# A hybrid mixer on one core: the rest of the input projection placed between the steps of the recurrence, and two attention stages given their own banks

## The chip, the cores and the metric

The kernel runs on one core of a Trainium2 chip. The metric is the device time of one execution in microseconds (us). Engines are named as in the profile: PE is TensorE (matrix products; PEld its weight loads), DVE is VectorE, ACT ScalarE, POOL GpSimd, SP SyncE, which issues most DMAs. PEclk is the share of TensorE's full clock that was granted.

## The reference, cut to what matters

One layer: 1024 latent and 256 context tokens, width 1024. The normalised tokens go through one input projection, whose columns feed three mixers side by side: a bidirectional recurrence (4 heads), a neighbourhood attention (8 heads) and a gated short convolution. Their outputs are concatenated and projected; then an expert mixer of 16384 experts follows.

```python
pc = split_columns(hc @ w_in)          # 256 context tokens
pl = split_columns(hl @ w_in)          # 1024 latent tokens
y_rw_c, y_rw_l = rwkv_mixer(pc, pl, ...)
y_na_l = neighbourhood_attention(ql, kl, vl, kc, vc, na_rpb)
y_sc_l = gated_short_conv(*pl[9:12], sc_conv_w)
yl = jnp.concatenate([y_rw_l, y_na_l, y_sc_l], axis=-1) @ w_out
...
xl = xl + g1 * yl
hl2 = rmsnorm(xl, norm2_g[i]) * (1.0 + sc2) + sh2
xl = xl + g2 * peer_ffn(hl2, ...)      # query projection, top-16 of keys, gathered or dense experts
```

The recurrence reads only the first nine column blocks of the projection (128 columns each), the attention and the convolution the other eighteen.

## The kernel before, in words

**Order of the work.** The program is written through a layer that puts each engine's instructions in an order of its own: what is written earlier has precedence, and what is written later fills in where an engine would be free and its buffers are there. Each engine then runs its own queue strictly in that order. So the place at which a piece of work is written decides where it stands in the queues.

**Projection.** `proj(m, blk, evac)` makes column block m for a block of tokens (`TBLK`: 0 with 256 tokens, 256 and 768 with 512 each). It loads 512 KB of weights, casts them on ACT into a rounded part `wh` (L206), subtracts on POOL for the rest `wl` (L208), and runs 8 x 3 products on PE into a tile `pj` (L158 to L160). The result goes to DRAM. `load_h` brings a block's normalised tokens back and splits them the same way (`hbh` on ACT L188, `hbl` on POOL L189). The loads of weights, of tokens and of modulation rows (`awT`) share two buffers.

**Recurrence.** `batch(step, d)` handles 256 tokens in direction d: for two pairs of heads the decays (`th`, `de`, `di`, `pe`, `pi`), on POOL `bb` and `kb` (L533, L534), 64 x 64 products on PE (all on L460: `pk`, `pr`, `tr`, `lkv`), then a triangular inverse, which starts with 15 steps of small DVE instructions (`yb`, `Y`, L576 to L580) and ends in `XT`, and last the chain of states (`mc`, `M`, `yc`). Ten batches are written one after the other; the projections that the recurrence itself needs (`rwkv_inputs`) stand between the first of them. The last use of a token block also normalises and writes the output (`y`, `yd`, `yo`). `yc` and `yo` have the only bank of kind ch.

**The other projections.** `head_inputs` (12 projections of a latent block, 8 of the context) and `conv_inputs` (6) are written after the recurrence, for block 256 and then 0, and in the trace some of them already run in its gaps. Those of block 768 are written much later, after group 0.

**Attention.** `attend` goes through heads and query blocks of 128 tokens. An item is: scores `pw` and `pc` on PE, maximum on DVE (L778 to L781), two exponentials on ACT (L782, L783), transposes `pt` on PE (L792), copies `pT` on ACT, the products `po` (L798), and a scaling `yn` on DVE (L799). Query blocks 0 and 1 come first, with all PSUM tiles in the two banks of kind pj; then group 0 (output projection of the first 256 tokens, normalisation, query projection of the experts, sorting of the keys' scores on DVE, L922 to L926); then query blocks 2 to 5, with every second item followed by a projection of block 768, and beside them the first 30 gathered expert rows (`ru`, DVE L1118); then the convolution, group 1, and the expert products up to the end.

Of the kernel before, what the change touches and what calls it, by code (L numbers as in the profile page):

```python
# [25 lines left out]
TBLK = ((0, 256), (256, 512), (768, 512))  # L26
# [28 lines left out]
def hybrid_kernel(ctx: ExitStack, tc: tile.TileContext, A: dict, out: bass.AP, dbg=None):  # L55
# [7 lines left out]
    def pool(name, bufs=1, side="left"):  # L63
        return tc.tile_pool(name=name, bufs=bufs, side=side, reuse_waits="tile")
# [106 lines left out]
    def drain(gen):  # L171
        for _ in gen:
            pass
# [288 lines left out]
    def batch(step, d):  # L462
# [14 lines left out]
        for h in range(2):  # L477
# [86 lines left out]
            for u in range(4):  # L564
# [3 lines left out]
            S[h] = dict(E=EL[:, :, 0, :], bn=G[:, :, 0, :], bp=G[:, :, 1, :], bb=G[:, :, 0:2, :], kt=G[:, :, 2, :], gk=G[:, :, 3, :],  # L568
                        rx=rx, krd=krd, vS=vS, tot=tots, gt=gt)

        nc.vector.tensor_copy(Y, id16.unsqueeze(1).to_broadcast([P, 8, 16]))
# [12 lines left out]
        for u in range(8):  # L584
            heads2(ps[:, u * 64:u * 64 + 64], (XT[:, u, :], stk))
        nc.scalar.copy(X, v8(ps))

        for l in range(2):
            ps = bank(f"lp_{step}{d}{l}", "rb")
            for u in range(8):  # L590
                heads2(ps[:, u * 64:u * 64 + 64], (S[u // 4]["E"][:, u % 4, :], X[:, u, :]))
            pm = gp.tile([P, 8, 64], F32, tag="pm", name=f"pm_{step}{d}{l}", bufs=2)
            nc.vector.tensor_mul(pm, v8(ps), mask(C_L16 + l, 8))
            ps = bank(f"lt_{step}{d}{l}", "rb")
            for u in range(8):
                heads2(ps[:, u * 64:u * 64 + 64], (pm[:, u, :], XT[:, u, :]))
            if l == 0:
                ps2 = bank(f"lx_{step}{d}{l}", "rb")
                for u in range(8):
                    heads2(ps2[:, u * 64:u * 64 + 64], (XT[:, u, :], pm[:, u, :]))  # L600
                nc.vector.tensor_add(X, v8(ps2), X)
            nc.vector.tensor_add(XT, v8(ps), XT)
        for h in range(2):
            s, ci = S[h], 2 * d + h
            x12 = s["gt"]("x12", [P, 4, 2, 64], 4)
            ps = bank(f"x12_{step}{ci}", "rb")
            for u in range(4):
                heads2(ps[:, u * P:(u + 1) * P], (XT[:, 4 * h + u, :], s["rx"][:, u].rearrange("p a b -> p (a b)")))
            nc.scalar.copy(x12, ps.rearrange("p (c a b) -> p c a b", c=4, a=2))
            s["x12"] = x12  # L610
        for h in range(2):
            s, ci = S[h], 2 * d + h
            pr = s["gt"]("pr", [P, 4, 2, 64], 4)
            na_ = 2 if lat else 1
            ps = bank(f"pr_{step}{ci}", "rb")
            for u in range(4):
                heads2(ps[:, u * P:u * P + 64 * na_], (s["x12"][:, u, 0, :], s["bb"][:, u, :na_, :].rearrange("p a b -> p (a b)")))
            nc.vector.tensor_add(pr[:, :, :na_, :], ps.rearrange("p (c a b) -> p c a b", c=4, a=2)[:, :, :na_, :], s["krd"][:, :, 0:na_, :])
            s["pr"] = pr

        ych = bank(f"yc_{step}{d}", "ch") if lat else None
# [55 lines left out]
        nc.sync.dma_start(d_y[:, 0:2, tl:tl + 256], gs)  # L677

    batch(0, 0)
    batch(0, 1)  # L680
    rwkv_inputs(TBLK[1])
    batch(1, 0)
    load_h(*TBLK[2], 0)
    rwkv_inputs(TBLK[2])
    batch(1, 1)
    for step in range(2, 5):
# [3 lines left out]
    st_c.close()  # L690


    left = iter(range(16, 48))
    load_h(*TBLK[1], 1)
    drain(head_inputs(TBLK[1], 3))
    drain(conv_inputs(TBLK[1]))
    load_h(*TBLK[0], 1)
    drain(head_inputs(TBLK[0], 2))
    st_w.close()
# [111 lines left out]

    with pool("na", 2, "right") as na:
        drain(attend(na, range(0, 2), 0, 512, ("pj", "pj", "pj", "pj"), (2, 2, 1, 2, 1)))
    st_k = ExitStack()
    tk = st_k.enter_context(pool("tk", 1, "right"))

    st_i = ExitStack()
# [24 lines left out]
    def group(gi, tp_, eng):  # L842
# [23 lines left out]
        def to_rows(dst, t0, nt):  # L866
            for tt in range(nt):
                for q in range(2):
                    ps = bank(f"xt{gi}{tt}{q}", "ra")
                    for j in range(4):  # L870
# [4 lines left out]

        pq = bank(f"s2{gi}", "ra")[:, :n]
        for k in range(KD):
# [19 lines left out]
        for hp2 in range(16):  # L897
# [7 lines left out]
            nc.scalar.copy(qh, ps)  # L905
            ps = bank(f"sc{gi}{hp2}", "ra")
            for tt in range(nt):
# [257 lines left out]

    st_w = ExitStack()
    W[0] = st_w.enter_context(pool("wst2", 2, "right"))
    WT[:] = du, ("u", "uh", "ul"), 3
    with pool("tp") as tp_:
# [4 lines left out]
        drain(topk(0, 4, 4))  # L1174
    load_h(*TBLK[2], 2)

    def heads():
        hin = itertools.chain(head_inputs(TBLK[2]), conv_inputs(TBLK[2]))
        for i in range(4):
            yield next(hin)  # L1180
        with pool("nb1") as na:
            for i, ev in enumerate(attend(na, range(2, 6), 0, 1024, ("ra", "rb", "ch", "ra"), (3, 2, 1, 1, 1))):
                yield ev
                if i % 2:
                    next(hin, None)

    beside(heads(), 36, *PACE["b1"])
    st_w.close()
    conv(256, TL)
# [260 lines left out]
```

## Time and profile before

| | us |
|---|---|
| median of 3 runs (lowest to highest) | 3749.64 (3747.22 to 3761.19) |
| the profiled execution | 3754.22 |
| its span, from the first to the last instruction | 3752.5 |
| PE busy | 3329.1 (89%) |
| DVE busy | 2810.7 (75%) |
| ACT busy | 1529.2 (41%) |
| POOL busy | 1378.3 (37%) |

Busy time is a mean over stages with different limits, so the stages are read one by one: the busy time of each engine in a stretch, the groups of instructions in it by source line and tile (with count, busy us, mean ns of one, the idle time of the engine before them and what ended it), and a tile's own row, with the shortest, median and longest duration and the start of the first and last. In names, `out<-in` are the program's tiles. PE's matrix products overlap each other, so many of them take less time than their mean duration times their count.

### The profile page before, as it was taken

To read this page: it belongs to the slowest core of one execution; us is meant where nothing else is said; L and a number is where in the kernel's file an instruction comes from. 1 tells how busy PE (TensorE), PEld (TensorE's weight loads), DVE (VectorE), ACT (ScalarE), POOL (GpSimd) and SP (SyncE) were. 2 spreads that over 40 slices of the span, in tenths; PEclk is the share of its full clock that TensorE was granted. 3 is DMA by queue.
4 is the path that set the end of the run, shared out by engine and by line. 5 is a ranking of instruction groups with operands and counts; after the bars stand their busy time and mean duration, and the time that the engine had idled before them with its cause. 6 is when DMAs were issued, how large, how long until landed. Compare 5 with 4: busy or idle time off the path is not lost.

```text
span 3752.5 us, 63457 instructions
## 1 busy us (share of the span) xinstructions
PE 3329.1 (89%) x23959; PEld 2970.6 (79%) x23959; DVE 2810.7 (75%) x6095; ACT 1529.2 (41%) x2934; POOL 1378.3 (37%) x1060
## 2 busy tenths in 40 slices
PE   7787877857879887989989999999988999999997
PEld 6576776645768766888989999999987788888886
DVE  6553657433495656979879999999877788888888
ACT  3443222223434433336443676666632323323332
POOL 3333111220044223355442425565443344444444
PEclk9899988965789878989999999999999999999998
DMA  6435422252366644699977879999999999999997
GB/s 246 134 96 154 122 83 71 84 174 70 105 199 180 183 161 162 221 325 302 328 265 258 296 253 361 352 354 368 347 356 308 329 342 350 339 352 333 338 353 244
DMA packets 405811, 928.56 MB, mean 247 GB/s; under 512 B 45568, under 2 KB 182144, under 8 KB 399872
## 3 DMA queue, kind: packets, MB, share of 16 engines
q1 hardware_dynamic: 248064, 408.81, 33.8%
q0 software_dynamic: 111920, 407.95, 30.2%
q10 hardware_dynamic: 45520, 107.76, 7.5%
q8 instruction: 188, 3.08, 0.3%
q14 instruction: 119, 0.97, 0.1%
HBM read 802.74 MB, written 121.63 MB: 246 GB/s over the span
## 4 chain that ended last, share of the span: by engine, by line
PE 33%; DVE 14%; issue 6%; DMA 5%; ACT 2%; POOL 1%; SPq 0%; ACTq 0%; DVEq 0%; POOLq 0%
PE dp L158 5%; PE dp L160 5%; PE dp L159 5%; DVE ru L1118 4%; PE ds L160 3%; PE ds L158 3%; PE ds L159 3%; PE dq L158 2%; PE dq L159 2%; PE dq L160 2%; PE gm L1033 2%; DMA ru<-in_peer_u_dram,idx 1%; DVE acc L1129 1%; DVE ob L1025 1%; DVE oa L1020 1%
## 5 line engine op out<-in xcount | busy, mean ns | idle before, releaser
L1101 POOL DMA_INDIRECT ru<-in_peer_u_dram,idx x384 | 515.2, 1342 | 740.8 <-ACT dqs L1353 171.8
L1101 POOL DMA_INDIRECT rv<-in_peer_v_dram,idx x384 | 511.5, 1332 | 688.6 <-ACT dqs L1353 228.3
L1118 DVE CUSTOM_DVE_ANT_0 ru<-ru,h 128x1024 f32<-128x1024 f32 x384 | 478.6, 1259 | 83.0 <-DMA ru<-in_peer_u_dram,idx 81.0
L1129 DVE SCALAR_TENSOR_TENSOR acc<-rv,gw,acc 128x1024 f32<-128x1024 f32 x381 | 488.9, 1283 | 38.9 <-DMA rv<-in_peer_v_dram,idx 32.7
L159 PE MATMUL dp<-dvls,dwhs 128*128 128x512 f32 x896 | 348.5, 389 | 1.1 <-DVE dvls L1235 1.1
L160 PE MATMUL dp<-dvhs,dwls 128*128 128x512 f32 x896 | 345.8, 389 | 0.0
L158 PE MATMUL dp<-dvhs,dwhs 128*128 128x512 f32 x896 | 316.9, 392 | 0.0
L208 POOL TENSOR_TENSOR wl<-w,wh 128x1024 fp32r<-128x1024 f32 x68 | 165.9, 2442 | 284.5 <-ACT wh L206 273.9
L158 PE MATMUL pj<-hbh,wh 128*128 128x512 f32 (+1 forms) x544 | 225.7, 415 | 43.7 <-ACT wh L206 30.7
L160 PE MATMUL pj<-hbh,wl 128*128 128x512 f32 (+1 forms) x544 | 219.3, 403 | 7.7 <-POOL wl L208 7.6
L159 PE MATMUL pj<-hbl,wh 128*128 128x512 f32 (+1 forms) x544 | 220.0, 404 | 3.7 <-POOL hbl L189 3.7
L1268 ACT ACTIVATE ge<-ds 128x256 f32<-128x256 f32 (+1 forms) x256 | 110.8, 433 | 235.4 <-PE ds L160 190.7
L1238 ACT CAST dwhs<-dws 128x640 fp32r<-128x640 f32 x128 | 91.7, 730 | 260.4 <-DVE dws L1237 129.6
L158 PEld LDWEIGHTS dp<-dvhs,dwhs 128*128 128x128 f32 x896 | 169.7, 189 | 35.2
L159 PEld LDWEIGHTS dp<-dvls,dwhs 128*128 128x128 f32 x896 | 168.3, 188 | 36.6 <-DVE dvls L1235 1.5
L160 PEld LDWEIGHTS dp<-dvhs,dwls 128*128 128x128 f32 x896 | 168.3, 188 | 35.0
L158 PE MATMUL dq<-dvhs,dwhs 128*128 128x512 f32 x384 | 150.9, 393 | 19.3 <-ACT dvhs L1234 15.2
L158 PEld LDWEIGHTS pj<-hbh,wh 128*128 128x128 f32 x544 | 114.6, 211 | 66.6 <-ACT wh L206 31.6
L1235 DVE TENSOR_TENSOR dvls<-dvs,dvhs 128x1024 fp32r<-128x1024 f32 x128 | 155.7, 1221 | 10.7 <-ACT dvhs L1234 10.0
L1033 PE MATMUL gm<-oa,ob 128*128 128x128 f32 x1280 | 158.5, 277 | 5.7 <-DVE oa L1020 5.2
L1033 PEld LDWEIGHTS gm<-oa,ob 128*128 128x128 f32 x1280 | 154.0, 193 | 7.2 <-issue 7.0
L1353 ACT COPY dqs<-dq 128x512 f32<-128x512 f32 x90 | 52.8, 586 | 257.4 <-PE dq L160 257.4
(1984 smaller groups left out, 10156.9 us busy)
## 6 DMA issues: line engine op xcount, KB each, us to landing
du<-in_peer_ut_dram SPq DMA_DIRECT2D x128, 512.0 KB
dvs<-in_peer_v_dram SPq DMA_DIRECT2D x128, 512.0 KB
d_ge<-ge ACTq DMA_DIRECT2D x128, 320.0 KB
d_g<-gt ACTq DMA_DIRECT2D x40, 1024.0 KB
dgs<-d_g SPq DMA_DIRECT2D x32, 1280.0 KB
dws<-d_ge SPq DMA_DIRECT2D x128, 320.0 KB
w<-in_w_in_dram SPq DMA_DIRECT2D x68, 512.0 KB
wq<-in_q_w_dram SPq DMA_DIRECT2D x48, 512.0 KB
```

Of the source, the lines that this page charges most:

```text
L158: nc.tensor.matmul(ps, lh_, rh_, start=start, stop=False)
L159: nc.tensor.matmul(ps, lh_, rl_, start=False, stop=False)
L160: nc.tensor.matmul(ps, ll_, rh_, start=False, stop=stop)
L208: WE[0].tensor_tensor(wl, w, wh.bitcast(F32), op=OP.subtract)
L1033: nc.tensor.matmul(ps[:, t * P:(t + 1) * P], ob[:, q + t], oa[:, q + t], start=True, stop=True)
L1101: paced(nc.gpsimd.indirect_dma_start(out=r, out_offset=None, in_=A[tab], in_offset=bass.IndirectOffsetOnAxis(ap=idx[:, tt, s:s + 1], axis=0)))
L1118: yield from rows("peer_u", tt, lambda s, u: nc.vector.tensor_tensor_reduce(u, u, h2, 1.0, 0.0, OP.mult, OP.add, act[:, s:s + 1]))
L1129: nc.vector.scalar_tensor_tensor(acc, v, w[:, s:s + 1], acc, op0=OP.mult, op1=OP.add)
L1235: sv = nc.vector.tensor_tensor(vl, v, vh.bitcast(F32), op=OP.subtract)
L1238: nc.scalar.copy(wh, wt)
L1268: ev = nc.scalar.activation(ge[:, t0:t0 + n], ps, AF.Gelu_apprx_tanh)
L1353: pace[0] = nc.scalar.copy(dqs[:, r % 2], ps)
```

## The change

- `others()` makes one sequence of all remaining projections: block 768 first (its tokens are still in place, so one reload goes), then 256, then 0. `fill()` takes the next of them, and `batch` calls it six times: after each pair of heads, after `x0`, after each of the two steps that complete the inverse, and after `pr`. It works from batch (1, 1) on, seven batches, so 42 of the 44 projections are written inside the recurrence; what is left follows it. The modulation rows are spread anew over them (2, 1 and 2 a call instead of 3 and 2), 32 as before.
- The attention of query blocks 0 and 1 gets its own space (its pool is opened after the pool `tk` of the sorting instead of giving its space to it), three score buffers instead of two, and banks of three kinds: ra for scores, pj for transposes, ch for outputs.
- Group 0 uses the two banks of kind rb throughout, where it had three ra banks as well.
- The attention of query blocks 2 to 5 no longer alternates with projections, and has its transposes in pj instead of rb, in a pool on the other side of memory. It is paced as 32 pieces instead of 36.

```diff
             S[h] = dict(E=EL[:, :, 0, :], ...)
+            fill()
...
         nc.scalar.copy(X, v8(ps))
+        fill()
...
             nc.vector.tensor_add(XT, v8(ps), XT)
+            fill()
...
             s["pr"] = pr
+        fill()
...
+    left = iter(range(16, 48))
+    def others():
+        for blk, na, i in ((TBLK[2], 2, None), (TBLK[1], 1, 1), (TBLK[0], 2, 1)):
+            if i is not None:
+                load_h(*blk, i)
+            yield from head_inputs(blk, na)
+            if blk[0]:
+                yield from conv_inputs(blk)
+    rest, fill = others(), lambda: None
...
     rwkv_inputs(TBLK[2])
+    fill = lambda: next(rest, None)
     batch(1, 1)
...
-    left = iter(range(16, 48))
-    load_h(*TBLK[1], 1)
-    drain(head_inputs(TBLK[1], 3))
-    drain(conv_inputs(TBLK[1]))
-    load_h(*TBLK[0], 1)
-    drain(head_inputs(TBLK[0], 2))
+    drain(rest)
...
-    with pool("na", 2, "right") as na:
-        drain(attend(na, range(0, 2), 0, 512, ("pj", "pj", "pj", "pj"), (2, 2, 1, 2, 1)))
     st_k = ExitStack()
     tk = st_k.enter_context(pool("tk", 1, "right"))
+    with pool("na", 2, "right") as na:
+        drain(attend(na, range(0, 2), 0, 512, ("ra", "pj", "ch", "ra"), (3, 2, 1, 2, 1)))
...
-        pq = bank(f"s2{gi}", "ra")[:, :n]
+        pq = bank(f"s2{gi}", "ra" if gi else "rb")[:, :n]
...
-    load_h(*TBLK[2], 2)
     def heads():
-        hin = itertools.chain(head_inputs(TBLK[2]), conv_inputs(TBLK[2]))
-        for i in range(4):
-            yield next(hin)
-        with pool("nb1") as na:
-            for i, ev in enumerate(attend(na, range(2, 6), 0, 1024, ("ra", "rb", "ch", "ra"), (3, 2, 1, 1, 1))):
-                yield ev
-                if i % 2:
-                    next(hin, None)
-    beside(heads(), 36, *PACE["b1"])
+        with pool("nb1", 1, "right") as na:
+            yield from attend(na, range(2, 6), 0, 1024, ("ra", "pj", "ch", "ra"), (3, 2, 1, 1, 1))
+    beside(heads(), 32, *PACE["b1"])
```

What the change makes of the queues is seen at three places. The first is POOL in the recurrence, between the two pairs of heads of batch (2, 1); `bb_210` and `bb_211` belong to the first and the second pair, and a `wl` with the number of its column block to a projection. Before:

```order
L533 TENSOR_TENSOR bb_210_4170<-x2_210_4148,pi_210_4161 128x256
L534 TENSOR_TENSOR kb_210_4171<-x4_210_4149,pi_210_4161 128x256
L208 TENSOR_TENSOR wl10_7493<-w10_7489,wh10_7491 128x1024
L510 MEMSET de_301_4856 128x4
L510 MEMSET di_301_4857 128x4
L533 TENSOR_TENSOR bb_211_4288<-x2_211_4266,pi_211_4279 128x256
```

And now:

```order
L533 TENSOR_TENSOR bb_210_4654<-x2_210_4632,pi_210_4645 128x256
L534 TENSOR_TENSOR kb_210_4655<-x4_210_4633,pi_210_4645 128x256
L208 TENSOR_TENSOR wl20_4375<-w20_4371,wh20_4373 128x1024
L208 TENSOR_TENSOR wl12_4466<-w12_4462,wh12_4464 128x1024
L208 TENSOR_TENSOR wl23_4741<-w23_4737,wh23_4739 128x1024
L208 TENSOR_TENSOR wl25_4891<-w25_4887,wh25_4889 128x1024
L208 TENSOR_TENSOR wl21_4992<-w21_4988,wh21_4990 128x1024
L510 MEMSET de_301_5617 128x4
L510 MEMSET di_301_5618 128x4
L533 TENSOR_TENSOR bb_211_4805<-x2_211_4783,pi_211_4796 128x256
```

Five projections' subtractions stand ahead of the second pair's `bb`, where one stood.

The second place is PE at the start of the attention of query blocks 0 and 1; the first digit behind a name is the head, the second the query block. Before, the second item's scores stand behind the first one's products:

```order
L792 MATMUL pt014_8450<-cst2_95,s01_8425 128x128 x2
L798 MATMUL po01_8454<-vN00_8366,pT01_8443 128x64 x6
L772 MATMUL pw10_8481<-kh10_8463,qs10_8465 128x256
L773 MATMUL pw10_8481<-kl10_8473,qs10_8465 128x256
L776 MATMUL pc10_8484<-kh10_8463,qs10_8465 128x256
```

Now two items' scores stand together, between products of the recurrence's last batch (`yc`, `mc`):

```order
L460 MATMUL yc_41_8732<-x12_411_8660,G_411_8288 64x64 x2
L782 MATMUL pw00_9027<-kh00_9009,qs00_9011 128x256
L786 MATMUL pc00_9030<-kh00_9009,qs00_9011 128x256
L782 MATMUL pw01_9066<-kh00_9009,qs00_9011 128x256
L783 MATMUL pw00_9027<-kl00_9019,qs00_9011 128x256
L787 MATMUL pc00_9030<-kl00_9019,qs00_9011 128x256
L786 MATMUL pc00_9030<-kh00_9009,qs00_9011 128x256
L787 MATMUL pc00_9030<-kl00_9019,qs00_9011 128x256
L783 MATMUL pw01_9066<-kl00_9019,qs00_9011 128x256
L460 MATMUL yc_41_8732<-M_333_7093,pr_410_8671 64x64 x2
```

The third place is PE in group 0's query projection, at the end of `q00` and its scores `sc00`. Before, another query projection stands beside it:

```order
L159 MATMUL q00_9648<-hl0_9592,wq00h_9644 128x256
L160 MATMUL q00_9648<-hh0_9591,wq00l_9646 128x256
L159 MATMUL q01_9702<-hl0_9592,wq01h_9698 128x256
L160 MATMUL q01_9702<-hh0_9591,wq01l_9700 128x256
L908 MATMUL sc00_9677<-keys00_9673,qh00_9675 128x128 x2
L158 MATMUL q02_9752<-hh0_9591,wq02h_9748 128x256
```

Now items of the attention of query blocks 2 to 5 stand between the two:

```order
L159 MATMUL q00_10281<-hl0_10225,wq00h_10277 128x256
L160 MATMUL q00_10281<-hh0_10224,wq00l_10279 128x256
L808 MATMUL po12_11449<-vN0256_11217,pT12_11437 128x64 x4
L802 MATMUL pt130_11480<-cst2_95,s13_11461 128x128 x3
L808 MATMUL po12_11449<-vN0256_11217,pT12_11437 128x64 x3
L802 MATMUL pt130_11480<-cst2_95,s13_11461 128x128
L802 MATMUL pt134_11486<-cst2_95,s13_11461 128x128 x3
L782 MATMUL pw22_11617<-kh2256_11599,qs2256_11601 128x384
L918 MATMUL sc00_10310<-keys00_10306,qh00_10308 128x128 x2
L158 MATMUL q01_10335<-hh0_10224,wq01h_10331 128x256
```

On DVE, from the weights of group 1's fourth output block (`wo13l`) on, the rows are those of before with hardly a difference. Lines of the changed kernel are ten higher than those of before in the attention and group 0.

More of the change, by code (lines that the diff above doesn't have):

```diff
@@ L868, in to_rows @@
                 for q in range(2):
-                    ps = bank(f"xt{gi}{tt}{q}", "ra")
+                    ps = bank(f"xt{gi}{tt}{q}", "ra" if gi else "rb")
                     for j in range(4):
@@ L905, in group @@
             nc.scalar.copy(qh, ps)
-            ps = bank(f"sc{gi}{hp2}", "ra")
+            ps = bank(f"sc{gi}{hp2}", "ra" if gi else "rb")
             for tt in range(nt):
@@ L1164, in beside @@
         gbase[0] = g0 + ng
-    st_w = ExitStack()
-    W[0] = st_w.enter_context(pool("wst2", 2, "right"))
-    WT[:] = du, ("u", "uh", "ul"), 3
     with pool("tp") as tp_:
@@ L1174, in hybrid_kernel @@
         drain(topk(0, 4, 4))
-    load_h(*TBLK[2], 2)
     def heads():
-        hin = itertools.chain(head_inputs(TBLK[2]), conv_inputs(TBLK[2]))
-        for i in range(4):
-            yield next(hin)
-        with pool("nb1") as na:
-            for i, ev in enumerate(attend(na, range(2, 6), 0, 1024, ("ra", "rb", "ch", "ra"), (3, 2, 1, 1, 1))):
-                yield ev
-                if i % 2:
-                    next(hin, None)
-    beside(heads(), 36, *PACE["b1"])
-    st_w.close()
+        with pool("nb1", 1, "right") as na:
+            yield from attend(na, range(2, 6), 0, 1024, ("ra", "pj", "ch", "ra"), (3, 2, 1, 1, 1))
+    beside(heads(), 32, *PACE["b1"])
     conv(256, TL)
```

## Prediction, made before the changed kernel was run

> **What bounds the kernel now.** I read the span first, then the busy time by stretch, then inside each stretch the groups of instructions and what their engine waited for. The first row is the span. The others are stretches (us from the start): length, busy us (instructions) of PE, weight loads, DVE, ACT and POOL, then granted clock, DMA share and GB/s.
>
> ```profile
> core 0: 3752.5 us, clock 0.922
> ...
> 345.00:690.00 345.00, 270.30 (x4924) 238.73 (x4925) 222.46 (x721) 97.90 (x214) 56.12 (x60) 0.88 0.31 94
> 690.00:815.00 125.00, 86.72 (x794) 73.50 (x792) 39.22 (x76) 28.34 (x48) 35.89 (x54) 0.82 0.48 151
> 815.00:969.00 154.00, 106.83 (x433) 86.59 (x433) 47.98 (x159) 46.77 (x122) 14.47 (x8) 0.52 0.26 75
> 969.00:1075.00 106.00, 88.49 (x656) 84.16 (x655) 77.61 (x311) 51.55 (x94) 16.30 (x15) 0.89 0.52 154
> 1075.00:1146.00 71.00, 58.12 (x240) 46.76 (x241) 57.95 (x164) 23.09 (x40) 38.17 (x21) 0.83 0.71 218
> 1146.00:1294.00 148.00, 133.42 (x810) 118.36 (x808) 91.76 (x222) 74.26 (x158) 56.96 (x31) 0.92 0.59 176
> 1294.00:1357.00 63.00, 51.12 (x279) 47.61 (x279) 38.24 (x115) 24.12 (x59) 13.82 (x11) 0.69 0.54 177
> 1357.00:1558.00 201.00, 169.51 (x733) 134.05 (x734) 140.51 (x483) 63.00 (x90) 54.20 (x44) 0.89 0.53 173
> 1558.00:3752.00 2194.00, 2088.22 (x12381) 1919.55 (x12379) 1902.92 (x3417) 972.58 (x1851) 977.68 (x719) 0.98 0.91 323
> ```
>
> Stretch by stretch this is: the recurrent mixer with some projections in its gaps (345 to 690), mostly projections of blocks 256 and 0 (690 to 815), the attention of query blocks 0 and 1 alone (815 to 969), group 0 (969 to 1075), the projections of block 768 and the attention of query blocks 2 to 5 (1075 to 1357), group 1, and the expert products. The last stretch has PE busy for 95% of it. Up to 1357 no engine is full, and that is where the change works.
>
> The attention from 815 to 969 is a chain, one item (a head and a query block) after the other:
>
> ```profile
> L792 PE MATMUL pt<-cst,s 128*128 128x128 f32 x96 | 28.1, 430 | 30.4 <-ACT s L782 29.9 <-ACT s L783 0.3
> ...
> L782 ACT ACTIVATE s<-pc,m 128x256 f32<-128x256 f32 x16 | 7.6, 473 | 42.6 <-DVE m L781 39.9 <-DMA d_y<-yt 2.4
> ...
> L799 DVE TENSOR_SCALAR yn<-po,m 128x64 f32<-128x64 f32 x16 | 4.5, 284 | 56.7 <-PE po L798 56.7
> ...
> L799 DVE TENSOR_SCALAR yn<-po,m x16: 283/284/284, 833.1 to 968.9; 128x64 f32<-128x64 f32 x16
> ```
>
> PE waits for ACT's exponentials, ACT for DVE's maximum, DVE for PE's products. PE, the busiest, works for 69% of the stretch, at a clock of 0.52. The last row gives the pace: sixteen items end between 833.1 and 968.9, so 135.8 / 15 = 9.05 us each, after a lead of 18 us.
>
> **Part A, the projections move into the recurrence.** How much they cost on PE, and how much room there is:
>
> ```profile
> 345.00:690.00 345.00, 81.02 (x296) 58.25 (x297) 0.00 (x0) 7.01 (x12) 0.88 0.31 94
> 690.00:815.00 125.00, 67.90 (x330) 56.40 (x328) 1.38 (x2) 5.29 (x12) 0.82 0.48 151
> 1075.00:1294.00 219.00, 119.34 (x432) 87.53 (x432) 1.37 (x2) 9.39 (x16) 0.89 0.63 190
> 551.00:555.00 4.00, 3.95 (x17) 3.11 (x17) 0.00 (x0) 0.00 (x0) 1.00 0.37 100
> ...
> 225.00:325.00 100.00, 94.90 (x1234) 75.59 (x1233) 37.61 (x109) 43.38 (x80) 28.45 (x21) 0.98 0.32 97
> ...
> PE x L460 <- DVE XT L580: 28.0, 6, 6.3
> PE pk L460 <- POOL bb L533: 12.6, 8, 6.4
> ```
>
> The first four rows count the projections' products (tile pj) alone. Blocks 256 and 0 already have theirs between 345 and 815 (296 + 330 of them). What comes in is block 768: 432 products, 18 projections of 24. Back to back at full clock one takes 3.95 / 17 = 0.232 us, so a projection is 5.6 us and the 18 are 100 us of PE. PE is busy for 270.30 + 86.72 = 357 of the 470 us, a share of 0.76; with the 100 it has to be 457. Were the share to stay at 0.76, the stretch would last 601 us (+131). The fifth row, where the mixer runs among its own input projections, reaches 0.95, which gives 481 (+11). I take 0.90, the share of 1146 to 1294, where projections fill the waits of another latency chain (133.42 / 148): 508 us, **+38**. The last two rows are the waits there are to fill: PE stands still until DVE has the inverse's XT, or until POOL has bb.
>
> Of the three reloads of h, block 768's goes. Block 256's, which stood ahead of 345, comes into the mixer, with eight subtractions in front of a bb on POOL; what that costs is saved ahead of 345, so I count it at nothing, and at 8 x 1.27 = 10 us if the mixer has to wait for it:
>
> ```profile
> L189 POOL TENSOR_TENSOR hbl<-hf,hbh x8: 1256/1270/2148, 1062.0 to 1075.1; 128x512 fp32r<-128x512 f32 x8
> ```
>
> The moved projections bring more than PE work: 18 casts on ACT, 18 weight subtractions (wl) on POOL, 18 weight loads of 512 KB and their spills on SP's and ACT's queues. ACT is busy for a quarter of the stretch, and DMA has a share of 0.31, so these hide. POOL's do not quite. A wl stands in POOL's queue ahead of bb and kb, for which PE waits, and DVE is held while it runs:
>
> ```profile
> L577 DVE TENSOR_TENSOR yb<-yb,E x105: 166/224/2219, 359.3 to 681.7; 128x8 f32<-128x8 f32 x7, 128x16 f32<-128x16 f32 x7, 128x24 f32<-128x24 f32 x7, 128x32 f32<-128x32 f32 x7
> ...
> 671.23 2.22 DVE L577 TENSOR_TENSOR yb<-yb,E 128x40 f32<-128x40 f32 x1
> ...
> 671.01 2.38 POOL L208 TENSOR_TENSOR wl<-w,wh 128x1024 fp32r<-128x1024 f32 x1 [10.10 <-PE pj L160]
> ```
>
> A multiply that takes 0.22 us in the median took 2.22 us under a wl that ran from 671.01 to 673.39. It is a step of the inverse, on the mixer's chain. If a third of the 18 meet such a step and cost 2 us each, that is **+12**; the ends are 0 and 18 x 2.38 = 43. The Trainium skill's "GPSIMD Engine Reference", section "1. Specifications", speaks against the change here: it says that GpSimd shares its SBUF interfaces with VectorE, with contention for DVE instructions that have two SBUF inputs. Taken at its widest, every wl would hold such an instruction, the term would be the 43 above rather than 12, and the forecast 31 later, 3681. The row shows the hold; a median of 224 ns says that most of these steps miss it.
>
> A is +38 + 12 = **+50**: the projections end at about 865 instead of 815. Between +11 and +174.
>
> **Part B, attention 0 and 1 in its own space and banks.** Before, all four kinds of PSUM tile took turns in the two pj banks with two score buffers; now scores, transposes and outputs have banks of three kinds and three score buffers, and PE's order lets a second item's scores stand ahead of the first one's transposes. The nearest rows are those of the later attention, which has that already, once it is alone:
>
> ```profile
> 1294.00:1357.00 63.00, 3.14 (x12) 0.69 0.54 177
> ```
>
> Twelve items ended there in 63 us, 5.25 us each, with 896 keys each, while here they have 768. With that pace, 18 + 15 x 5.25 = 97 us, **-57**. The lead I keep at 18: the first loads hide under the last batch of the mixer now, but the outputs need the ch bank, which that batch's results hold until it ends. The ends: 154 if the pace stays (0), and PE's 106.83 us at clock 0.52 turned into 56 us at full clock, plus the lead, 74 (-80).
>
> **Part C, the attention of query blocks 2 to 5 beside group 0.** With the projections gone, what is left between 969 and 1357 is group 0 and 32 items. PE loses 119.34 us of products, so DVE is the next limit: 77.61 + 57.95 + 91.76 + 38.24 = 265.6 us. Two things leave:
>
> ```profile
> L382 DVE TENSOR_TENSOR zc<-pj,zc 128x512 f32<-128x512 f32 x2 | 1.4, 686 | 0.5 <-PE pj L160 0.5
> ...
> L1118 DVE CUSTOM_DVE_ANT_0 ru<-ru,h 128x1024 f32<-128x1024 f32 x33 | 51.3, 1558 | 33.1 <-DMA ru<-in_peer_u_dram,idx 33.0
> L718 DVE SCALAR_TENSOR_TENSOR cs<-cu,cvw,cs 128x768 f32<-128x768 f32 x4 | 4.0, 1009 | 0.0
> L719 DVE TENSOR_TENSOR cs<-cz,cs 128x768 f32<-128x768 f32 x2 | 1.9, 953 | 0.0
> L716 DVE TENSOR_SCALAR cs<-cu,cvw 128x768 f32<-128x768 f32 x2 | 1.2, 617 | 2.2 <-DMA d_y<-cs 2.2
> ...
> 1010.00:1075.00 65.00, 55.63 (x449) 54.70 (x448) 56.30 (x269) 29.22 (x58) 15.29 (x15) 0.95 0.56 166
> 1050.00:1075.00 25.00, 17.05 (x140) 16.45 (x138) 25.00 (x132) 11.75 (x26) 9.92 (x7) 0.93 0.55 155
> ```
>
> Without zc (1.4) and with the convolution's cs (7.1) behind the attention, DVE has 257 us left. In the query projections of group 0, where it sorts, its share is 56.30 / 65 = 0.87, and for 25 us it is full. I take 0.87: 295 us, **-93**. At a full DVE it would be 257 (-131). If nothing overlapped, group 0's 106, the 57.95 of DVE in the sorting and first gathers behind it, and 32 x 5.25 = 168 make 332 (-56). The 33 us in which DVE waited for gathered rows stay a risk, since the thirty gathers now crowd behind the sort. Two rb banks now serve all of group 0; its chain of projection, scores and eviction has DVE's time to hide in.
>
> **What follows 1357** has the same rows in the same order, and PE at 95%: what is gained before it arrives at the end whole.
>
> **The sum** is against the profiled execution's own 3754.2 us (the span of 3752.5 and 1.7 around it): +50 - 57 - 93 = -100, so 3654. That execution lay 4.6 above the median of the runs, so I predict **3650**.
>
> **Rivals.** (1) *PE's queue is blocked by projections that wait for their weights: slower.* The order puts a projection at fixed places; if its weights are not there, the mixer's steps behind it wait too. For it:
>
> ```profile
>   ACT wh L206: 48.7, 8
> ...
>   POOL wl L208: 13.4, 9
> ```
>
> So long did PE stand before projections between 345 and 815, until their weights were cast or split; loads of w, h and the modulation rows share two buffers. In 690 to 815, where little else fills, PE's share was 86.72 / 125 = 0.69. At that share over the whole, A is 662 - 470 + 12 = +204 and the kernel ends at 3804. It decides from a share of 0.73 downwards, where 457 / 0.73 = 626 makes A +168 and the sum +18. Against it: from 225 to 325 the same two kinds of work reach 0.95.
>
> (2) *The gain is eaten: no change.* The share stays at 0.76: A is +131 + 12 and the sum -7, 3743. As much, 3744, comes out with A at +50, B at 0 and C at its worst, -56; but PE's order has an item between each two query projections.
>
> (3) *The clock rises: faster still.* At 815 to 969 it is 0.52 and at 1294 to 1357 0.69; 225 to 325, dense, has 0.98. If overlap brings full clock, A is +11, B -80 and C -93: -162, 3588. The Trainium skill's "TensorE: Matmul & The Clock Gate", section "Part 1: The HAM clock gate", has such a rule: half clock after an idle window of about 3.4 us, full after a busy one. By that rule, denser stretches would come out so; the 0.69 at the very pace I use for B says that two items at a time are not dense enough.
>
> **How the numbers follow.** About 0.5%, 19 us, is what a measurement of this kernel can tell from no change: faster ends at 3731, slower begins at 3768. The forecast, with its terms between 3600 and 3720, has 0.63; (3) 0.15; (2) 0.15, half of it under 3731; (1) 0.07. The range 3590 to 3725 leaves out the far part of (3), most of (2) and all of (1). Faster 0.85, same 0.08, slower 0.07.
>
> **What would show it.** Right: the projections end at 845 to 890 with PE's share about 0.9 and no pj behind; the first sixteen yn at 5 to 6.5 us; group 1's first product some 290 to 300 us after attention 1, with DVE's share near 0.87; the rest as long as now. Wrong: long waits of the mixer's products behind wh or wl, a pace of yn still near 9, DVE idle among gathers, or an expert stretch longer than 2194 us.

## The result, and the profile after

| | before | after |
|---|---|---|
| median of 4 runs (lowest to highest), us | 3750.81 (3747.22 to 3761.19) | 3642.15 (3637.34 to 3653.76) |
| the profiled execution, us | 3754.22 | 3643.33 |
| its span, us | 3752.5 | 3641.6 |

The ratio is 0.971, with a 95% interval of 0.968 to 0.9741: 108.7 us less. Forecast were 3650, from 3590 to 3725. The stretches of the changed kernel, cut where the same stages now end (length, busy us and instructions of PE, weight loads, DVE, ACT and POOL, then clock, DMA share, GB/s):

```profile
345.00:842.00 497.00, 430.26 (x5831) 366.44 (x5831) 267.16 (x755) 149.44 (x295) 140.89 (x106) 0.93 0.39 119
842.00:894.00 52.00, 28.67 (x368) 24.46 (x363) 24.78 (x69) 14.08 (x35) 8.40 (x37) 0.73 0.47 123
894.00:950.00 56.00, 50.15 (x380) 47.20 (x380) 35.81 (x134) 37.75 (x101) 7.29 (x4) 0.91 0.59 179
950.00:1105.00 155.00, 135.91 (x1059) 131.24 (x1059) 120.97 (x458) 92.40 (x195) 20.61 (x13) 0.94 0.55 158
1105.00:1218.00 113.00, 78.06 (x476) 71.33 (x474) 98.56 (x338) 46.61 (x111) 49.84 (x37) 0.73 0.66 204
1218.00:1251.00 33.00, 0.56 (x2) 0.27 (x2) 11.08 (x19) 2.30 (x4) 0.94 (x1) 0.50 0.63 214
1251.00:1441.00 190.00, 164.79 (x735) 132.09 (x736) 135.55 (x469) 61.07 (x87) 52.92 (x42) 0.93 0.53 175
1441.00:3641.00 2200.00, 2089.26 (x12378) 1916.24 (x12376) 1903.74 (x3424) 964.98 (x1845) 978.32 (x720) 0.98 0.91 322
```

They are the mixer with all projections (up to 842), the mixer's own end, attention 0 and 1, group 0 with the attention of query blocks 2 to 5 (two rows), a stretch of 33 us in which PE has next to nothing to do, group 1, and the expert products. The rows of the tiles that mark the ends (duration ns min/median/max, first to last start):

```profile
L158 PE MATMUL pj<-hbh,wh x101: 278/283/632, 711.1 to 840.9; 128*128 128x256 f32 x64, 128*128 128x512 f32 x37
...
L460 PE MATMUL yo<-cst,yd x128: 218/289/366, 665.9 to 889.9; 64*64 64x64 f32 x128
...
L809 DVE TENSOR_SCALAR yn<-po,m x16: 271/283/285, 893.6 to 949.4; 128x64 f32<-128x64 f32 x16
...
L809 DVE TENSOR_SCALAR yn<-po,m x32: 260/278/285, 985.1 to 1217.9; 128x64 f32<-128x64 f32 x32
...
L158 PE MATMUL o<-h2h,wo10h x8: 389/389/792, 1250.9 to 1262.2; 128*128 128x512 f32 x8
```

Group 1's first product stood at 1360.5 before, as the same row of the kernel before has it:

```profile
L158 PE MATMUL o<-h2h,wo10h x8: 389/389/795, 1360.5 to 1375.5; 128*128 128x512 f32 x8
```

So by that point 109.6 of the 110.9 us of span are won, and what follows is as long as it was: from there to the end of the span it is 2390.7 us, where it was 2392. By marks: the last of the sixteen yn moved from 968.9 to 949.4, -19.5 (forecast A + B: -7); from there to group 1's first product it was 391.6 and is 301.5, -90 (forecast C: -93). In the recurrence nearly nothing waits for weights any more (engine, line and what it waited for: us, times, longest):

```profile
PE x L460 <- DVE XT L581: 15.4, 3, 7.8
PE pk L460 <- POOL bb L533: 10.0, 3, 5.8
...
PE x L460 <- DVE XT L604: 5.7, 1, 5.7
...
PE pj L160 <- POOL wl L208: 0.8, 1, 0.8
PE pj L158 <- ACT wh L206: 0.7, 1, 0.7
```

The projections' own waits are 1.5 us in sum, where the same two made 29.9 before (24.0 behind wh and 5.9 behind wl, from 345 to 815); what is left is the mixer's chain. The 33 us without PE work have one cause in the waits, and the timeline (start, us, engine, line, tile) shows the chain behind it:

```profile
PE o L158 <- ACT h2h L867: 32.2, 1, 32.2
```

```profile
1218.28 0.33 SPq L723 DMA_DIRECT2D cu<-d_u  x1
...
1240.65 0.32 SPq L730 DMA_DIRECT2D d_y<-cs  x1
...
1241.70 1.83 SPq L866 DMA_DIRECT2D yk<-d_y  x3
...
1250.91 0.79 PE L158 MATMUL o<-h2h,wo10h 128*128 128x512 f32 x1 [32.17 <-ACT h2h L867]
```

The convolution's load of `cu` starts only behind the last yn at 1217.9, the result of its second half leaves at 1240.7, and group 1's input `yk` is loaded behind it on SP. Before, the same wait was 2.7 us (kernel before):

```profile
PE o L158 <- ACT h2h L857: 2.7, 1, 2.7
```

### The profile page after: what moved, and what is told of

Same layout as the page of the kernel before. It is cut to its first block, busy times and chain, and to the rows that moved or that the text cites. A ratio compares the mean times of both kernels' runs of the same rounds, so it can differ in the third digit from the quotient of the medians.

```text
span 3641.6 us, 63347 instructions
## 1 busy us (share of the span) xinstructions
PE 3260.1 (90%) x23959; PEld 2915.8 (80%) x23959; DVE 2795.1 (77%) x6095; ACT 1514.4 (42%) x2920; POOL 1370.4 (38%) x1052
## 4 chain that ended last, share of the span: by engine, by line
PE 38%; DVE 14%; issue 8%; DMA 6%; POOL 2%; ACT 2%; SPq 0%; ACTq 0%; another core or an unknown queue 0%; DVEq 0%; POOLq 0%
PE ds L160 5%; PE ds L158 5%; PE ds L159 5%; PE dp L158 4%; PE dp L160 4%; PE dp L159 4%; DVE ru L1128 4%; PE gm L1043 3%; PE dq L158 2%; PE dq L159 2%; PE dq L160 2%; DMA ru<-in_peer_u_dram,idx 1%; DVE acc L1139 1%; DMA rv<-in_peer_v_dram,idx 1%; PE po L808 1%
## 5 line engine op out<-in xcount | busy, mean ns | idle before, releaser
L1128 DVE CUSTOM_DVE_ANT_0 ru<-ru,h 128x1024 f32<-128x1024 f32 x384 | 469.2, 1235 | 54.5 <-DMA ru<-in_peer_u_dram,idx 54.4
L158 PE MATMUL pj<-hbh,wh 128*128 128x512 f32 (+1 forms) x544 | 218.1, 401 | 13.7 <-ACT hbh L188 10.8
L159 PE MATMUL pj<-hbl,wh 128*128 128x512 f32 (+1 forms) x544 | 212.1, 390 | 3.7 <-POOL hbl L189 3.7
L160 PE MATMUL pj<-hbh,wl 128*128 128x512 f32 (+1 forms) x544 | 211.4, 389 | 1.2 <-POOL wl L208 1.2
L1233 ACT CAST dvhs<-dvs 128x1024 fp32r<-128x1024 f32 x128 | 133.3, 1052 | 60.7 <-DMA dvs<-in_peer_v_dram 60.1
```

Of the source, the lines that this page charges most:

```text
L158: nc.tensor.matmul(ps, lh_, rh_, start=start, stop=False)
L159: nc.tensor.matmul(ps, lh_, rl_, start=False, stop=False)
L160: nc.tensor.matmul(ps, ll_, rh_, start=False, stop=stop)
L1128: yield from rows("peer_u", tt, lambda s, u: nc.vector.tensor_tensor_reduce(u, u, h2, 1.0, 0.0, OP.mult, OP.add, act[:, s:s + 1]))
L1233: nc.scalar.copy(vh, v)
```

## The experiments

All edits but the fifth are made in the changed kernel. Each time stands beside runs of the kernel before on the same chip, whose medians were 3743 to 3748; the ratio is to those. The change itself stood beside runs with a median of 3750.81, so by the ratios each of these kernels compares with the change 3 to 7 us worse than the differences of medians below.

The edits act before the expert products, whose stretch has scatter of its own. So the table gives the first start of `ds`, the experts' first product, in the profiled execution, what that is against the change, and the length of the rest:

| | median, us | `ds` starts, us | against the change | from there to the end, us |
|---|---|---|---|---|
| before | 3750.81 | 1559.0 | +117.7 | 2193.5 |
| the change | 3642.15 | 1441.3 | | 2200.3 |
| 1, convolution's buffers | 3617.44 | 1429.4 | -11.9 | 2196.2 |
| 2, projections behind | 3679.97 | 1489.6 | +48.3 | 2186.4 |
| 3, pj banks again | 3686.63 | 1485.1 | +43.8 | 2195.4 |
| 4, wl on DVE | 3599.92 | 1413.1 | -28.2 | 2172.7 |
| 5, old kernel, new attention | 3664.59 | 1471.4 | +30.1 | 2193.3 |
| 6, po in rb | 3630.15 | 1430.4 | -10.9 | 2202.5 |
| 7, 1 and 4 | 3607.96 | 1412.9 | -28.4 | 2197.3 |
| 8, group 0 in ra | 3662.5 | 1470.3 | +29.0 | 2185.5 |
| 9, 4 and 6 | 3614.88 | 1411.2 | -30.1 | 2197.9 |
| 10, 10 rows | 3616.84 | 1402.3 | -39.0 | 2209.5 |
| 11, 1, 4 and 10 | 3571.26 | 1375.2 | -66.1 | 2192.1 |
| 12, 1, 4 and no row | 3598.01 | 1356.3 | -85.0 | 2240.8 |

### 1. The convolution's buffers on the other side

```diff
     def conv(t0, t1):
-        with pool(f"cv{t0}", 1, "right") as cvp:
+        with pool(f"cv{t0}", 1, *(("right",) if t0 == 0 else ())) as cvp:
```

> The buffers of the convolution of tokens 256 to 1023 lie where group 0's were, on the left, instead of in the space that the attention of query blocks 2 to 5 gives back. Theory (the 33 us without PE work from 1218 to 1251 come from that space: the convolution's loads wait for the attention's end, and group 1 for the convolution): PE's longest wait ahead of group 1's first o falls from 32.2 us to under 8, and the kernel gains 22 to 30 us, about 3615. Rival (DVE bounds the stretch, so its 6 us of cs and the rows of y only come out elsewhere): within 8 us of 3642.

Measured: 3617.44, ratio 0.9652 (0.962 to 0.9685) where the change itself has 0.971. PE's wait at group 1's start, and then the marks:

```profile
PE o L158 <- ACT h2h L867: 2.8, 1, 2.8
```

```profile
L809 DVE TENSOR_SCALAR yn<-po,m x32: 264/276/285, 986.2 to 1232.0; 128x64 f32<-128x64 f32 x32
...
L158 PE MATMUL o<-h2h,wo10h x8: 389/391/796, 1235.6 to 1251.2; 128*128 128x512 f32 x8
```

The wait of 32.2 us is gone, so the space was its cause: the change put the attention's pool on the right, where the convolution's buffers come to lie in it. But group 1 starts only 15.3 us earlier, since the last yn is now 14 us later. The medians differ by 25 us, the two profiled executions by 16 (3627.4 and 3643.3), and `ds` starts 12 us earlier. Half of what was won at one place came back at the other. The convolution's cs, 7.1 us, now run on DVE from 1157 to 1192, ahead of that last yn; what makes the other 7 us is not shown.

### 2. The projections written behind the recurrence

```diff
     rwkv_inputs(TBLK[2])
-    fill = lambda: next(rest, None)
     batch(1, 1)
```

> The six calls of fill() give nothing; all 44 projections are written behind the ten batches, as the old kernel had most of them, but with block 768's among them. Everything else is as changed. Theory (the place in the order is what fills PE's waits): PE's share from 345 to the last pj falls from 0.87 to about 0.76, which puts the last pj at 900 to 950, and the kernel comes to 3690 to 3745. Rival (the order fills the gaps by itself, and only the move of block 768 out of the later stage counts): last pj within 20 us of 841, kernel within 15 us of 3642.

Measured: 3679.97, ratio 0.9829 (0.9795 to 0.9862), 38 us above the change. The stretch from 345 to the last projection, and where that stands:

```profile
345.00:912.00 567.00, 448.90 (x6109) 390.69 (x6110) 260.50 (x779) 155.52 (x302) 136.74 (x136) 0.88 0.35 111
```

```profile
L158 PE MATMUL pj<-hbh,wh x544: 277/389/1415, 46.2 to 911.8; 128*128 128x512 f32 x144, 128*128 128x256 f32 x38
```

PE's share is 448.90 / 567 = 0.79, and the last projection starts at 911.8 instead of 841. The place in the written order is worth 38 us in the medians and 48 at `ds`; the order does not fill the gaps by itself as well. The time is 10 us under the expected range.

### 3. Attention 0 and 1 in the pj banks again

```diff
-        drain(attend(na, range(0, 2), 0, 512, ("ra", "pj", "ch", "ra"), (3, 2, 1, 2, 1)))
+        drain(attend(na, range(0, 2), 0, 512, ("pj", "pj", "pj", "pj"), (2, 2, 1, 2, 1)))
```

> The attention of query blocks 0 and 1 has all its PSUM tiles in the two pj banks again, with two score buffers; its space and everything else are as changed. Theory of the prediction (banks and buffers set the pace): the sixteen yn come at 7 to 9 us each instead of 3.7, the last one at 1000 to 1030, and the kernel is 35 to 80 us slower, since group 0's products can fill a part. Rival (the pace comes from group 0's and the recurrence's products beside it, and from the clock that they keep up): the yn stay under 5 us each and the kernel within 15 us of 3642.

Measured: 3686.63, ratio 0.9847 (0.9813 to 0.9881), 44 us above the change:

```profile
L809 DVE TENSOR_SCALAR yn<-po,m x16: 277/283/284, 866.1 to 1001.9; 128x64 f32<-128x64 f32 x16
...
L802 PE MATMUL pt<-cst,s x90: 272/421/476, 871.4 to 998.3; 128*128 128x128 f32 x90
```

```profile
866.00:1002.00 136.00, 99.73 (x518) 80.93 (x517) 55.13 (x177) 46.67 (x119) 12.53 (x39) 0.59 0.30 90
```

135.8 / 15 = 9.05 us an item, to the hundredth the old pace, although the attention has its own space and group 0's first products stand beside it. The banks and the score buffers set the pace; the edit changes both, so it does not say which of the two does. The first yn comes 27 us earlier than in the change (866.1 against 893.6): nothing waits for the ch bank.

### 4. The weights' subtraction on DVE

```diff
-    fill = lambda: next(rest, None)
+    fill = lambda: next(rest, None)
+    WE[0] = nc.vector
...
     drain(rest)
+    WE[0] = nc.gpsimd
```

> From batch (1, 1) to the last projection the weights' subtraction wl runs on DVE instead of POOL. Theory of the prediction (wl on POOL stands ahead of bb and kb and holds DVE's small steps, some 12 us): POOL's waits go, the yb keep their 0.22 us, and the kernel gains 5 to 15 us. Rival (44 subtractions of about 1.2 us now stand in DVE's own queue, on the chain of the inverse): 20 to 50 us slower.

Measured: 3599.92, ratio 0.9613 (0.9581 to 0.9644), 42 us under the change in the medians, where the first theory expected 5 to 15. DVE from 345 to 842 by groups (count, busy us, mean ns, idle time before them), in the change:

```profile
L578 DVE TENSOR_TENSOR yb<-yb,E 128x8 f32<-128x8 f32 (+14 forms) x105 | 33.3, 317 | 2.9
L579 DVE TENSOR_TENSOR Y<-Y,yb 128x8 f32<-128x8 f32 (+14 forms) x105 | 32.3, 307 | 3.0
```

and with wl on DVE, followed by the whole stretch and PE's waits in it:

```profile
L208 DVE TENSOR_TENSOR wl<-w,wh 128x1024 fp32r<-128x1024 f32 x42 | 52.0, 1238 | 63.6 <-ACT wh L206 63.2 <-PE yo L460 0.2
...
L578 DVE TENSOR_TENSOR yb<-yb,E 128x8 f32<-128x8 f32 (+14 forms) x105 | 24.0, 228 | 2.7
L579 DVE TENSOR_TENSOR Y<-Y,yb 128x8 f32<-128x8 f32 (+14 forms) x105 | 23.6, 225 | 2.9
```

```profile
345.00:842.00 497.00, 435.68 (x5897) 369.00 (x5897) 289.81 (x832) 155.88 (x311) 46.88 (x67) 0.93 0.42 129
```

```profile
PE pk L460 <- POOL bb L533: 12.5, 5, 5.2
...
PE x L460 <- DVE XT L604: 4.7, 3, 2.9
PE x L460 <- DVE XT L581: 3.6, 3, 1.7
```

The inverse's two groups fall from 65.6 to 47.6 us. Without the 52.0 us of wl, DVE needs 237.8 us where it needed 267.16 with fewer instructions done: the 42 wl on POOL (2378 ns in the median) had lengthened DVE's work by 29 us, 0.7 us each. PE's wait for XT falls from 21.1 to 8.3 us, while that for POOL's bb does not fall (10.0 and 12.5). So the price of a wl on POOL is the hold on DVE rather than POOL's queue. The last projection starts at 811.2, 30 us earlier, and `ds` 28 us earlier. The rest of the gain lies in the expert stretch (2173 us here), which the edit does not touch; why it was short is open.

### 5. The old kernel with nothing but the new attention 0 and 1

```diff
-    with pool("na", 2, "right") as na:
-        drain(attend(na, range(0, 2), 0, 512, ("pj", "pj", "pj", "pj"), (2, 2, 1, 2, 1)))
     st_k = ExitStack()
     tk = st_k.enter_context(pool("tk", 1, "right"))
+    with pool("na", 2, "right") as na:
+        drain(attend(na, range(0, 2), 0, 512, ("ra", "pj", "ch", "ra"), (3, 2, 1, 2, 1)))
```

> The old kernel with nothing but the attention of query blocks 0 and 1 changed: its own space, the banks ra, pj and ch, three score buffers. Theory (banks and buffers set the pace, and the clock follows the denser products): the sixteen yn come at 3.7 to 5.3 us instead of 9.05, and the kernel gains 55 to 80 us against the old one. Rival (without the recurrence's and group 0's products beside it the clock stays near 0.5): the pace is 6 to 8 us and the gain 15 to 45 us.

Measured: 3664.59, ratio 0.979 (0.9752 to 0.9828), 79 us under the kernel before:

```profile
L799 DVE TENSOR_SCALAR yn<-po,m x16: 272/284/285, 832.0 to 896.6; 128x64 f32<-128x64 f32 x16
...
L158 PE MATMUL o<-h2h,wo10h x8: 389/392/792, 1277.0 to 1292.8; 128*128 128x512 f32 x8
```

```profile
832.00:897.00 65.00, 58.38 (x399) 54.83 (x397) 33.88 (x141) 38.64 (x106) 10.89 (x6) 0.81 0.43 126
```

64.6 / 15 = 4.31 us an item. This part alone brings 79 of the 109 us. The last yn is at 896.6, 72 us earlier than before. From there, the projections moved into the recurrence put it at 949.4, 52.8 us later, and the shorter stretch behind takes them back and more: group 1 starts at 1250.9 instead of 1277.0.

### 6. The attention's outputs in another bank

```diff
-        drain(attend(na, range(0, 2), 0, 512, ("ra", "pj", "ch", "ra"), (3, 2, 1, 2, 1)))
+        drain(attend(na, range(0, 2), 0, 512, ("ra", "pj", "rb", "ra"), (3, 2, 1, 2, 1)))
```

> The changed kernel with the outputs po of the attention of query blocks 0 and 1 in the rb banks instead of the one ch bank. Theory (the 52 us between the last projection at 841 and the first yn at 893.6 are a wait for the ch bank, which the recurrence's last batch holds until 890): the first yn comes at 855 to 870, and the kernel gains 10 to 25 us. Rival (the outputs then share rb with the last batch's mc and group 0, or the last batch is slowed by the items among its products): within 8 us of 3642.

Measured: 3630.15, ratio 0.9699 (0.9661 to 0.9737), 12 us under the change in the medians, though the two ratios' intervals overlap:

```profile
L809 DVE TENSOR_SCALAR yn<-po,m x16: 265/277/285, 866.3 to 938.0; 128x64 f32<-128x64 f32 x16
```

The first yn comes 27 us earlier, so it was the ch bank that held it; the pace worsens from 3.72 to 4.78 us an item, and at the last yn 11.4 us are left; `ds` starts 10.9 us earlier.

### 7. Experiments 1 and 4 together

> The two gains together: the convolution's buffers on the left, and wl on DVE from batch (1, 1) to the last projection. Theory (they lie at different places of the path): the gains add, -25 and -42, so about 3575. Rival (DVE bounds what lies between, and the first eats the second): 3590 to 3605.

Measured: 3607.96, ratio 0.9636 (0.9595 to 0.9676): no better than experiment 4 alone, and 3 us over the rival's range. The experts' first product `ds` stands at 1412.9 here and at 1413.1 there. Without the convolution's move the last yn of query blocks 2 to 5 comes at 1191.0 and group 1 starts at 1222.6 (experiment 4); with it they stand at 1213.5 and 1217.1. The wait is gone, but the yn come 22 us later. The gains do not add.

### 8. Group 0 in the ra banks

```diff
-        pq = bank(f"s2{gi}", "ra" if gi else "rb")[:, :n]
+        pq = bank(f"s2{gi}", "ra")[:, :n]
```

(and so in `to_rows` and for the scores `sc`.)

> The changed kernel with group 0 in the three ra banks again, which the scores of the attention of query blocks 2 to 5 use too. Theory (items can stand beside group 0 only with banks of their own): fewer items lie within group 0, the last yn of query blocks 2 to 5 comes 15 to 40 us later than 1217.9 and the kernel is as much slower. Rival (DVE sets the stretch whatever the banks): within 8 us of 3642.

Measured: 3662.5, ratio 0.9796 (0.9756 to 0.9836), 20 us above the change:

```profile
L809 DVE TENSOR_SCALAR yn<-po,m x32: 261/279/285, 1077.9 to 1249.8; 128x64 f32<-128x64 f32 x32
```

The first item of query blocks 2 to 5 ends at 1077.9 instead of 985.1, the last one 32 us later. That items stand beside group 0 takes banks of their own.

### 9. Experiments 4 and 6 together

> The changed kernel with wl on DVE from batch (1, 1) to the last projection, and the outputs po of the attention of query blocks 0 and 1 in rb. Theory (the first shortens the recurrence, the second takes the attention off its end): both gains together, 42 and 12 us, about 3588. Rival (with the recurrence shorter there is less to wait for, and po in rb makes the yn slower): 3595 to 3605, no better than wl on DVE alone.

Measured: 3614.88, ratio 0.966 (0.9637 to 0.9682), no better than experiment 4 alone, and 10 us over the rival's range. The rival holds in the marks: the last yn comes 4 us earlier (919.3 against 923.6), and `ds` at 1411.2 against 1413.1.

### 10. Fewer gathered rows beside the attention

```diff
-PACE = dict(g0=5, b1=(30,), g1=(40,), u=430)
+PACE = dict(g0=5, b1=(10,), g1=(60,), u=430)
```

> The changed kernel with 10 instead of 30 gathered rows beside the attention of query blocks 2 to 5, and 60 instead of 40 beside group 1. Theory (DVE sets the stretch up to the end of that attention, as the prediction had it): the last yn of query blocks 2 to 5 comes 15 to 30 us earlier than 1217.9; how much of it stays depends on group 1, where the same 20 rows then lie: the kernel gains 0 to 20 us. Rival (DVE waits there for others, ACT's exponentials or PE, so its work is not the bound): the last yn within 8 us of 1217.9, and the kernel the same or slower.

Measured: 3616.84, ratio 0.9659 (0.9633 to 0.9686), 25 us under the change, where the theory had 0 to 20:

```profile
L809 DVE TENSOR_SCALAR yn<-po,m x32: 260/275/284, 981.5 to 1192.9; 128x64 f32<-128x64 f32 x32
```

```profile
PE o L158 <- ACT h2h L867: 30.7, 1, 30.7
```

The last yn is 25 us earlier, with the convolution's wait as long as in the change: 14 rows are done on DVE by then, 19.5 us, where the change has 33 and 43.5 us. DVE bounds this stretch. In the change it is all but full from 1060 to 1180, busy for 115.73 of 120 us:

```profile
1060.00:1180.00 120.00, 89.99 (x606) 85.73 (x605) 115.73 (x455) 50.31 (x115) 41.47 (x29) 0.76 0.65 203
```

`ds` starts 39 us earlier, since group 1 takes 178 us up to it instead of 190, although more rows lie beside it (46 instead of 35). Why it is shorter is not shown. Up to `ds` 60 rows are done where the change has 68, so a part of the gain there is work put off.

### 11. Experiments 1, 4 and 10 together

> Convolution's buffers on the left, wl on DVE, and 10 instead of 30 gathered rows beside the attention of query blocks 2 to 5. Theory (the two first gains did not add because the convolution's work then fell on a full DVE): with DVE relieved they do, 3570 to 3585. Rival (the rows only move into group 1 and cost there what they cost here): 3595 to 3610.

Measured: 3571.26 (3569.03 to 3572.51), ratio 0.9539 (0.9521 to 0.9558): faster than both kernels, 71 us under the change, and in the theory's range. `ds` starts 38 us earlier than in experiment 7:

```profile
L158 PE MATMUL ds<-h2h,du0h x16: 277/334/365, 1375.2 to 1383.5; 128*128 128x256 f32 x8, 128*128 128x384 f32 x8
```

This does not show that the convolution's move now counts. The 20 rows by themselves bring `ds` 39 us forward (experiment 10), as much as the 38 here, and experiments 4 and 10 alone add up to 28 + 39 = 67 us at `ds`, where the three together have 66. In the medians 42 + 25 = 67 of the 71 us are theirs. So that wl and the rows add is what these numbers say; the run with these two and without the convolution's move, which would tell what the move is worth beside them, was not made.

### 12. No gathered row beside the attention

Here the edit is shown against experiment 11.

```diff
-PACE = dict(g0=5, b1=(10,), g1=(60,), u=430)
+PACE = dict(g0=5, b1=(0,), g1=(70,), u=430)
```

> As the run before (convolution's buffers on the left, wl on DVE), with no gathered row beside the attention of query blocks 2 to 5 and 70 beside group 1. Theory (every row taken out of the stretch in which DVE is full is won, since group 1's first half has room): 10 rows of about 1.5 us, so 8 to 15 us under the 3571 of before, about 3560. Rival (group 1's second half, where DVE is full from 1300 to 1420, gets them back): 3567 or more.

Measured: 3598.01, ratio 0.9602 (0.9574 to 0.963), 27 us slower than experiment 11. Up to the experts the theory holds, behind that the rival and more:

```profile
1356.00:3597.00 2241.00, 2107.02 (x12407) 1935.25 (x12406) 1929.29 (x3529) 965.35 (x1847) 993.33 (x731) 0.97 0.89 319
```

```profile
PE pt L804 <- ACT s L794: 25.7, 4, 19.5
PE ds L160 <- DVE du5l L1058: 12.5, 1, 12.5
...
PE ds L160 <- DVE du6l L1058: 5.4, 1, 5.4
```

`ds` starts 19 us earlier (54 gathered rows are done by then, 60 in experiment 11), but the expert stretch takes 2241 us instead of the 2192 of experiment 11: its first products wait for du (weights that DVE splits) and its attention for ACT's s. The three waits make 43.6 us; from 1400 to 2690 in experiment 11, those behind s and du were 17.7 (7.8, 6.3 and 3.6). That explains 26 of the 49 us; the rest, and why s is late, stay open.

## Why the prediction was right, point by point

**The whole.** The sum of -100 came out as -110.9 in the profiled executions. The three terms have the right sign, and none is off by more than some 15 us. But in A and in C two errors each offset one another, so that the sum came so close is in part luck.

**A, +50.** Measured against experiment 5, which is the old kernel with the new attention: the first yn goes from 832.0 to 893.6, +61.6, the last from 896.6 to 949.4, +52.8. The size holds; the way there was not the one forecast. The step "the projections end at about 865" named too late an end: their last products start at 841, 39 us later than in the kernel before (801.9), where the step had 50. And the step "the lead I keep at 18" failed: from there the first yn took 52 us. The mixer's own last products now come behind the projections, yo up to 889.9, and hold the ch bank (experiment 6). From 345 to 894 PE is busy for 430.26 + 28.67 of 549 us, 0.84 where I took 0.90: the mixer's end, with no projection left beside it, has 0.55 from 842 to 894. The two errors offset each other.

**The wl's hold, +12 within A.** The inverse's yb and Y take 65.6 us instead of 55.7, the sum of 29.5 and 26.2 of the kernel before:

```profile
L577 DVE TENSOR_TENSOR yb<-yb,E 128x8 f32<-128x8 f32 (+14 forms) x105 | 29.5, 281 | 3.2
L578 DVE TENSOR_TENSOR Y<-Y,yb 128x8 f32<-128x8 f32 (+14 forms) x105 | 26.2, 250 | 3.3
```

That is +10, and 12 / 18 = 0.67 us a wl was the price that experiment 4 shows, 0.7. What the prediction did not draw from it: the wl that were there already paid the same, so that all 42 in the stretch were worth 30 us to the last projection and 28 to `ds`. The Trainium skill's "GPSIMD Engine Reference", section "1. Specifications", warned of this contention, and the trace agrees: the hold is real, at 0.7 us a wl and not at the full 2.38 that its widest reading would give.

**B, -57.** It was -72 by itself (968.9 to 896.6). The step that was off is the pace of 5.25 us, taken from a stretch at a clock of 0.69. Here PE is busy for 50.15 of 56 us at a clock of 0.91, a transpose takes 273 ns in the median where it took 421 with the old banks, and an item takes 55.8 / 15 = 3.72 us:

```profile
L802 PE MATMUL pt<-cst,s x78: 272/273/421, 897.5 to 946.3; 128*128 128x128 f32 x78
```

This was rival 3, the rising clock, for this one term, and its -80 matches the 135.8 - 55.8 between the first and the last yn. That the banks and score buffers do it and not the neighbours is experiment 3, with its pace of 9.05. The Trainium skill's "TensorE: Matmul & The Clock Gate", section "Part 1: The HAM clock gate", ties the clock to idle windows; the rows agree in direction: share 0.90 with clock 0.91 here, 99.73 / 136 = 0.73 with 0.59 in experiment 3.

**C, -93.** It was -90, with DVE as the limit that experiment 10 shows, but two steps failed and offset each other. The step that put "the convolution's cs (7.1) behind the attention" counted their work as saved and not the wait of group 1 for them: 32.2 us in which PE has next to nothing and DVE is busy for 11 of 33 us. And "DVE has 257 us left" was too much. From 969 to 1357 DVE had 812 instructions in 265.6 us; from 950 to 1251 it has 815, the convolution's among them, in 120.97 + 98.56 + 11.08 = 230.6. Largely the same instructions have become shorter, `qs` for one (before, then after):

```profile
L751 DVE TENSOR_TENSOR qs<-qd,qs 64x512 fp32r<-64x512 f32 x8 | 22.5, 2809 | 3.1 <-ACT qs L750 2.9
```

```profile
L761 DVE TENSOR_TENSOR qs<-qd,qs 64x512 fp32r<-64x512 f32 x8 | 13.8, 1724 | 5.3 <-ACT qs L760 4.9 <-issue 0.3
```

POOL's work in the same two stretches fell from 125.3 to 71.4 us, since the 18 wl have left. So the hold that the prediction priced where the wl went was probably paid here before; no run tests that by itself. Up to the last yn DVE is busy for 219.5 of 268 us, 0.82, where the forecast took 0.87. Without the wait (experiment 1) group 1 starts 1235.6 - 951.1 = 284.5 us behind the last yn of query blocks 0 and 1, between the 295 forecast and the bound of 257. The two rb banks for group 0 hide as forecast, and are what lets the items in: 20 us (experiment 8).

**Rivals 1 and 2** did not come. PE's waits for wh and wl are 1.5 us in sum. The gain of B was not eaten by A: with C the three make 109 where B alone makes 79. The stretch behind 1357 stayed as long, as forecast.

Open is why the expert stretch took between 2173 us (experiment 4) and 2241 us (experiment 12) in these kernels: how much of it is scatter of single executions and how much its own order. It matters: of the 42 us that experiment 4 gains, 28 stand ahead of the experts. Only for experiment 12 do waits explain a part.

## What to carry to other kernels

Price a moved piece of work by what it leaves bare where it was and whom it delays where it goes: here the attention behind the recurrence ended 53 us later and the recurrence's end lost its filling, and the later stage still gave back 90. When a pool changes its side, look for what used to get that space early; a wait of 32 us came from one such word, and it shows only as idle time ahead of the next product. Two gains on one path need not add: the convolution's move alone brought `ds` 12 us forward and, on top of the wl's, nothing. And before a gain is put down to one of several edits made together, the others have to be run without it: the best kernel here is as fast as two of its three edits explain.

## What the runs showed of the hardware

- A subtraction of 128x1024 on POOL (2.38 us) beside a DVE that works on SBUF lengthened DVE's own instructions by 0.7 us on the mean (29 us for 42 of them, experiment 4); steps of the inverse, 0.22 us in the median, took up to 2.5 us, and at most 0.7 us in that stretch with the subtractions on DVE. The same subtraction on DVE itself took 1.24 us, so here POOL's help cost more than half of what it took over.
- With two banks taking turns and two score buffers the attention's pace was 9.05 us in two kernels whose neighbouring work was different, at clocks of 0.52 and 0.59; with banks of three kinds and three score buffers it was 3.72 and 4.31 at 0.91 and 0.81. A transpose took 421 ns in the median with the first and 273 ns with the second.
